# Stores of keys and reciprocal rows moved from the SyncE queue to the ScalarE queue

## The chip, the cores and the metric

The kernel runs on one core of a Trainium2 chip. A core has five engines that run in parallel, each working through its own list of instructions in order: TensorE (PE: matrix products and transposes, results in PSUM), VectorE (DVE), ScalarE (ACT), GpSimd (POOL) and SyncE (SP), which computes nothing and issues DMA transfers between HBM and the on-chip SBUF. Engines wait for one another, and for transfers, through semaphores. A transfer is issued by an instruction in the list of some engine; an instruction whose wait is not yet met holds up all that stands behind it in that list.

The metric is the time of one execution on the device in microseconds (us). The kernel before took 1256.27 us as the median of 3 runs (1255.15 to 1257.36).

## The reference

One layer: `x + W_out(concat[A(h) * silu(g_a), B(h) * silu(g_b)])` with `h = RMSNorm(x)`, 2048 tokens, model width 1024, heads of 64, all in float32. One input projection gives queries, keys, values and gates of both mixers; queries and keys are RMS-normalised per head and rotated.

- Mixer A: 8 query heads on 2 key heads, causal window of 128 tokens, with a learned sink per head. Per query: `m = max(scores, sink)`, `p = exp(s - m)`, `l = sum(p) + exp(sink - m)`, `o = p v / l`.
- Mixer B: 8 heads, three causal patterns (window, dilation): (128, 1), (512, 4), (2048, 16). A query reads the keys `t - j*r`. The three outputs are merged by their softmax denominators: `sum_i w_i o_i / sum_i w_i`, with `w_i = l_i exp(m_i - max m)`.

So at the end of each softmax there is a division by a number per token and head: this is where the reciprocal rows come from.

## The kernel before, in words

**Precision.** A float32 product on TensorE is made of three products of split operands: a high part `h`, rounded by ScalarE as it copies, and a low part `l = x - h`. Each projection so takes three matmuls (`mm3`, L241 to L244), and keys are kept as a high tile `KK` and a low tile `KL` (`klz` in the profile).

**Stages.** `STAGES` (L26) runs through B0 to B3 (two heads of mixer B each), A0 and A1 (four query heads of mixer A each), O0 and O1 (halves of the output projection). By the profile the B stages last until about 665 us, the A stages until about 1070 us, and the output projection makes up the rest. Each stage has four blocks `sb` of 512 tokens, in two halves of 256.

**Projection** (`proj`, L246). For every 128 tokens, 24 matmuls collect into a PSUM tile `pj` (two buffers). ScalarE squares it (L410) and copies V's high part (L411), VectorE makes the rotation's products and V's low part (L311); then `pj` is free. GpSimd adds (L431) and makes the norm factors (L182), VectorE applies them (L447), and ScalarE and GpSimd split the result into high and low (L456 to L459). Loads of x (L148), of weights (L118, L131), rotation tables and scales are issued along the way.

**Finish** (`finish`, L342). Some time later these splits are transposed on TensorE (`qk_transposes`, L463). ScalarE copies out the high keys (L478 into `KK`) and the low keys (L502 into `KL`); GpSimd writes a second ordering of the queries (`qc`, L479). In a B stage the block's queries, high keys, low keys and gates are then stored to HBM (`qd`, `kd`, `ld`, `gd`; L360 to L369), one transfer per head, because the dilated patterns read them back in another order in the next stage. The carried last keys of a block are copied by ScalarE into the next one (L349, L352).

**Attention units.** `units_B`, `units_A` and `units_D` give pieces of work (scores, transposes, products with V, an `after` step) that `advance` (L931) places between the matmuls of the projection. `units_D` holds the dilated patterns of the stage before, for residue r = 0 to 3. Its `load` (L780) reads `qd`, `kd` (L785), `ld` (L788) and `vd` back.

**The reciprocal rows.** At the end of a dilated unit (`after`, L854) and of a pair of A heads (`rows`, L662), the merge weights or reciprocals are worked out as a small tile with one row per token. TensorE transposes it, ScalarE copies it out of PSUM (`rr`: L879 with 16 x 128, L673 with 8 x 128 numbers), and it is stored to a small HBM tensor (`rD`, L881; `rA`, L675). From there it is loaded again as a broadcast over 64 partitions (`Rb`, L890 and L682), and GpSimd multiplies the attention outputs by it (L899, L904; L688). A list `late` of counted-down steps keeps some pieces of other work between the store and the load, and between the load and the use.

**What sets the order.** The program is traced in Python order; a planner (`TileContext(nc, schedule_with_timeline_sim=True)`, L1036) then orders each engine's list by priority and by a simulated timeline, assigns buffers, and adds the semaphores. On the chip each list is run strictly in its planned order. In the kernel before, every transfer is issued by SyncE: one list for loads and stores alike.

## Time and profile before

| | |
|---|---|
| Median of 3 runs | 1256.27 us (1255.15 to 1257.36) |
| Profiled execution | 1261.51 us, of which 1259.4 us are the span from the first to the last instruction |
| TensorE busy | 1174.8 us (93%), mean granted clock 0.969 |
| VectorE, ScalarE, GpSimd busy | 850.7 (68%), 834.7 (66%), 680.4 us (54%) |
| DMA | 220.98 MB in 196883 packets; the queue's packets took 59.3% of the time of 16 DMA engines |
| Stores moved by the change | kd x32 (128 KB each), ld x32 (128 KB), rD x16 (8 KB), rA x16 (4 KB), all on the SyncE queue |

How to read the lines shown below: an engine's row in the page has its busy time, the share of the span and the number of instructions. In rows of waits, "SPq L890 <- DMA rD<-rr: 34.7, 14, 5.3" says that the SyncE queue, at the instruction of line 890, waited for the transfer into rD, 34.7 us in total, 14 times, 5.3 us at the longest. In rows in order of time the first number is the start and the second the duration, both in us; "[7.27 <-DMA Rb<-rD]" is the idle time before it and what ended it. A transfer's row on SPq is its issue: the time for which the instruction occupied SyncE. A row that begins with a time and "DMA" comes from the chain of waits, and shows a transfer from its issue to its landing. Names such as `po<-idr,hl` are output and inputs by the program's tile names.

### The profile page before, as it was taken

The numbers are of one execution on the slowest core, as the hardware profiler recorded it, in microseconds if no ns is written. First come the engines' busy times: TensorE is split into PE (matmuls) and PEld (weight loads), VectorE is DVE, ScalarE is ACT, GpSimd is POOL, SyncE is SP. The second block draws the span as 40 slices with busy tenths as digits, with TensorE's granted clock in tenths as the row PEclk, the third lists the DMA queues.
The fourth block names the chain that finished last, engine by engine and source line by source line (L and its number), as shares of the span: only waits on it lengthen the run. The fifth ranks groups of instructions, "written<-read, shape, count | busy, mean of one in ns | idle before, by whom it ended". The sixth has DMA issues, their size and how long they took to land.

```text
span 1259.4 us, 25438 instructions
## 1 busy us (share of the span) xinstructions
PE 1174.8 (93%) x8328; PEld 1141.3 (91%) x8328; DVE 850.7 (68%) x2288; ACT 834.7 (66%) x2418; POOL 680.4 (54%) x788
## 2 busy tenths in 40 slices
PE   6898979899899798899998999999999999999899
PEld 5898979899799798888997999898899998999898
DVE  5676768678677678776777788789868877522221
ACT  6477868678677687676777677677776776522221
POOL 4886734566645574536576567565655554333122
PEclk9899989999899899899998999999999999999999
DMA  7454677877687667687775764545333225566561
GB/s 215 120 166 127 193 226 212 229 200 212 182 250 207 210 190 201 189 244 204 199 210 172 228 203 143 150 137 167 114 97 94 80 89 165 163 192 211 166 191 69
DMA packets 196883, 220.98 MB, mean 175 GB/s; under 512 B 34312, under 2 KB 143632, under 8 KB 196752
## 3 DMA queue, kind: packets, MB, share of 16 engines
q1 hardware_dynamic: 196752, 219.37, 59.3%
q8 instruction: 66, 1.08, 0.4%
q14 instruction: 65, 0.53, 0.1%
HBM read 164.44 MB, written 54.86 MB: 174 GB/s over the span
## 4 chain that ended last, share of the span: by engine, by line
PE 55%; DMA 16%; DVE 10%; ACT 8%; POOL 6%; issue 3%; SPq 2%; POOLq 0%; ACTq 0%; DVEq 0%
PE pj L244 39%; DMA xs<-in_xT 3%; DMA Rb<-rD 2%; DMA stg<-in_wB 2%; PE po L849 2%; DMA stg<-in_wO 2%; DMA stg<-in_wA 2%; PE sc L590 1%; PE sc L591 1%; PE po L645 1%; PE pt L828 1%; PE po L735 1%; PE pt L719 1%; ACT P L599 1%; DVE ptl L574 1%
## 5 line engine op out<-in xcount | busy, mean ns | idle before, releaser
L244 PE MATMUL pj<-wh,xh 128*128 128x384 f32 (+1 forms) x1008 | 332.8, 332 | 12.2 <-ACT wh L104 5.5
L244 PE MATMUL pj<-wl,xh 128*128 128x384 f32 (+1 forms) x1008 | 334.4, 332 | 0.8 <-DVE wl L102 0.7
L244 PE MATMUL pj<-wh,xl 128*128 128x384 f32 (+1 forms) x1008 | 333.4, 331 | 1.3 <-DVE xl L157 1.3
L157 POOL TENSOR_TENSOR xl<-xs,xh 128x512 fp32r<-128x512 f32 x158 | 210.3, 1341 | 146.3 <-ACT xh L155 136.6
L155 ACT ACTIVATE xh<-xs 128x512 fp32r<-128x512 f32 x252 | 154.5, 629 | 123.6 <-PE pj L244 100.6
L244 PEld LDWEIGHTS pj<-wh,xh 128*128 128x128 f32 x1008 | 194.0, 193 | 15.7 <-ACT wh L104 5.8
L244 PEld LDWEIGHTS pj<-wl,xh 128*128 128x128 f32 x1008 | 194.8, 193 | 3.2 <-DVE wl L102 1.1
L244 PEld LDWEIGHTS pj<-wh,xl 128*128 128x128 f32 x1008 | 194.4, 193 | 3.0 <-DVE xl L157 1.6
L574 DVE TENSOR_TENSOR ptl<-pt,pth 128x512 fp32r<-128x512 f32 (+3 forms) x232 | 142.0, 619 | 35.5 <-ACT pth L573 31.8
L244 PE MATMUL pj<-xh,wgh 128*128 128x256 f32 x496 | 147.7, 298 | 17.9 <-DVE V L311 12.0
L244 PE MATMUL pj<-xh,wgl 128*128 128x256 f32 x496 | 145.8, 294 | 0.0
L244 PE MATMUL pj<-xl,wgh 128*128 128x256 f32 x496 | 145.4, 293 | 0.0
L573 ACT ACTIVATE pth<-pt 128x512 fp32r<-128x512 f32 (+3 forms) x232 | 123.1, 543 | 23.1 <-PE pt L719 8.1
L431 POOL TENSOR_TENSOR t<-t,t 128x256 f32<-128x256 f32 (+1 forms) x96 | 78.1, 814 | 77.9 <-DVE t L422 57.2
L244 PEld LDWEIGHTS pj<-xh,wgh 128*128 128x128 f32 x496 | 97.8, 197 | 19.7 <-ACT klz L502 5.9
L244 PEld LDWEIGHTS pj<-xl,wgh 128*128 128x128 f32 x496 | 97.8, 197 | 0.6
L244 PEld LDWEIGHTS pj<-xh,wgl 128*128 128x128 f32 x496 | 97.4, 196 | 0.9 <-DVE wgl L105 0.2
L814 ACT ACTIVATE P<-P,scD 128x256 f32<-128x256 f32 (+3 forms) x128 | 71.6, 560 | 33.6 <-DVE scD L813 32.9
L157 DVE TENSOR_TENSOR xl<-xs,xh 128x512 fp32r<-128x512 f32 x94 | 76.9, 823 | 21.1 <-ACT xh L155 20.5
L447 DVE TENSOR_TENSOR t<-t,fac 128x256 f32<-128x256 f32 (+1 forms) x96 | 67.4, 710 | 30.8 <-POOL fac L182 23.7
L182 POOL TENSOR_TENSOR fac<-un,mhalf 128x8 f32<-128x8 f32 (+1 forms) x48 | 85.4, 1779 | 2.5
L813 DVE CUSTOM_DVE_ANT_0 P<-sc,mk 128x256 f32<-128x256 f32 (+3 forms) x128 | 61.1, 484 | 32.2 <-PE sc L809 31.5
(188 smaller groups left out, 3082.8 us busy)
## 6 DMA issues: line engine op xcount, KB each, us to landing
xs<-in_xT SPq DMA_DIRECT2D x94, 512.0 KB
xs<-mx SPq DMA_DIRECT2D x32, 512.0 KB
vd<-V SPq DMA_DIRECT2D x64, 128.0 KB
qd<-qc SPq DMA_DIRECT2D x32, 256.0 KB
TT<-tab SPq DMA_DIRECT2D x32, 256.0 KB
cv<-vd SPq DMA_DIRECT2D x32, 256.0 KB
cq<-qd SPq DMA_DIRECT2D x32, 256.0 KB
ck<-kd SPq DMA_DIRECT2D x64, 128.0 KB
```

Source lines behind the costliest of these rows:

```text
L155: nc.scalar.activation(h, f, AF.Copy)
L157: eng.tensor_tensor(l, f, f32(h), op=OP.subtract)
L182: nc.gpsimd.tensor_tensor(y, u, mhalf.to_broadcast([128, n]), op=OP.pow)
L244: nc.tensor.matmul(o, a, b, start=first and n == 0, stop=last and n == 2, skip_group_check=True)
L431: nc.gpsimd.tensor_tensor(t1[:, :n], t1[:, :n], t2[:, :n], op=OP.add)
L447: nc.vector.tensor_tensor(t1v, t1v, fac[:, tt, :, None].to_broadcast([128, nh, 64]), op=OP.mult)
L573: nc.scalar.activation(hi, pt, AF.Copy)
L574: nc.vector.tensor_tensor(lo, pt, f32(hi), op=OP.subtract)
L590: nc.tensor.matmul(sc[:, j, :], q[h // 2][:, h % 2, i, :], kw, start=True, stop=False)
L813: nc.vector.tensor_tensor_reduce(pd, o[:, :m], m2[:, 512 - m:], -0.125, BIG, OP.add, OP.min, nb)
L814: nc.scalar.activation(pd, pd, AF.Exp, bias=nb, scale=-1.0, accum_out=l)
L849: nc.tensor.matmul(po[:, o:o + w], a, b, start=n_ == 0, stop=n_ == len(seq) - 1, skip_group_check=True)
```

## The change

Four of the issuing calls name another engine; nothing else differs. The 32 stores of high keys, the 32 stores of low keys, the 16 stores of merge weights and the 16 stores of A's reciprocals stand in ScalarE's list instead of SyncE's. The transfers themselves, their sizes and their readers are the same. The stores of queries (`qd`) and gates (`gd`), whose last writers are GpSimd and VectorE, and all loads stay with SyncE.

```diff
@@ finish, B stage
             for h in range(2):
                 nc.sync.dma_start(d["q"][h][:, :, cs].rearrange("r p c -> p r c"),
                                   f32(Q[si, sb][1][:, h]))
-                nc.sync.dma_start(d["k"][h][:, :, cs].rearrange("r p c -> p r c"),
+                nc.scalar.dma_start(d["k"][h][:, :, cs].rearrange("r p c -> p r c"),
                                   f32(KK[:64, h, :, 1:5, :]).rearrange("p r i u -> p r (i u)"))
             for h in range(2):
                 hs = slice(64 * h, 64 * h + 64)
-                nc.sync.dma_start(d["l"][:, hs, cs].rearrange("r p c -> p r c"),
+                nc.scalar.dma_start(d["l"][:, hs, cs].rearrange("r p c -> p r c"),
                                   f32(KL[hs, h, :, 1:5, :]).rearrange("p r i u -> p r (i u)"))
@@ rows, A stage
             nc.scalar.activation(rr[:8], pr, AF.Copy)
             d = dram([8, 128], f"rA{si}_{sb}_{p}")
-            nc.sync.dma_start(d, rr[:8])
+            nc.scalar.dma_start(d, rr[:8])
@@ after, dilated unit
                 nc.scalar.activation(rr, pr, AF.Copy)
                 dd = dram([16, 128], f"rD{si}_{r}")
-                nc.sync.dma_start(dd, rr)
+                nc.scalar.dma_start(dd, rr)
```

## The prediction

> **What bounds the kernel now.** I read the page first, then the stages, then what the queue's head and TensorE wait for, and last three places in order of time.

> ```profile
> span 1259.4 us, 25438 instructions
> PE 1174.8 (93%) x8328; PEld 1141.3 (91%) x8328; DVE 850.7 (68%) x2288; ACT 834.7 (66%) x2418; POOL 680.4 (54%) x788
> PE 55%; DMA 16%; DVE 10%; ACT 8%; POOL 6%; issue 3%; SPq 2%; POOLq 0%; ACTq 0%; DVEq 0%
> 0.00:665.00 665.00, 605.76 (x4072) 587.87 (x4073) 476.59 (x1267) 488.32 (x1399) 391.75 (x494) 0.95 0.70 199
> 665.00:1070.00 405.00, 386.87 (x2774) 373.75 (x2774) 319.59 (x922) 295.90 (x921) 237.64 (x255) 0.98 0.47 142
> ```

> TensorE is busy for 93% of the span, so 85 us at most can be won from its idle time. The two rows of stages (columns: length, busy time of PE, PEld, DVE, ACT, POOL, then clock, DMA share, GB/s) put 59 us of it into the four B stages (0 to 665 us) and 18 us into the A stages. ScalarE is 73% busy in both. In the chain the SyncE queue itself has 2%, some 25 us, and DMA in flight 16%: the issuing queue is seldom what is late, but what it issues often is.

> ```profile
> SPq L890 <- DMA rD<-rr: 34.7, 14, 5.3
> SPq L675 <- ACT rr L673: 28.7, 11, 4.6
> SPq L881 <- ACT rr L879: 10.9, 6, 2.6
> POOL o1c L899 <- DMA Rb<-rD: 58.3, 15, 8.2
> PE pj L244 <- DVE V L311: 13.2, 7, 5.7
> PE sc L808 <- DMA ck<-kd: 1.6, 1, 1.6
> ```

> The first three rows are the SyncE queue's waits (us in total, times, longest), the fourth is GpSimd's, the last two are TensorE's. SyncE stands 39.6 us at its head until ScalarE has written a reciprocal row (L675, L881), and then 34.7 us more until that row has landed in HBM, before it issues the broadcast load Rb (L890), for which GpSimd in turn waits 58.3 us.

> **The change, part by part.** First, what moves to ScalarE's instruction stream. Each issue occupies the engine that makes it:

> ```profile
> L362 SPq DMA_DIRECT2D kd<-KK x32: 602/619/1321, 68.2 to 686.5; - x32
> L366 SPq DMA_DIRECT2D ld<-klz x32: 574/598/1777, 69.6 to 687.8; - x32
> L675 SPq DMA_DIRECT2D rA<-rr x16: 284/290/517, 783.7 to 1099.9; - x16
> L881 SPq DMA_DIRECT2D rD<-rr x16: 328/358/660, 207.8 to 863.0; - x16
> ```

> (ns, minimum/median/maximum.) That is 32 x 0.619 = 19.8 us, 32 x 0.598 = 19.1, 16 x 0.290 = 4.6 and 16 x 0.358 = 5.7, together 49.3 us off SyncE and onto ScalarE. No row of before has an issue on ScalarE; from these rows it lies between 0.28 us, the shortest of the four forms, and 1.78 us, the longest. I take the medians, because the work of the issue is the same.

> Second, **what that delays**. Each of the 16 B blocks issues two high-key and two low-key stores: a burst of 2 x 0.619 + 2 x 0.598 = 2.43 us, right behind the copies that fill the key tiles. Three windows of 10 us that begin where these copies end:

> ```profile
> 218.10:228.10 10.00, 10.00 (x66) 9.76 (x65) 6.74 (x23) 7.41 (x26) 7.42 (x10) 1.00 0.86 249
> 391.50:401.50 10.00, 10.00 (x73) 9.83 (x72) 8.81 (x31) 9.88 (x34) 5.04 (x6) 1.00 0.64 184
> 567.30:577.30 10.00, 10.00 (x73) 9.81 (x72) 6.39 (x20) 8.78 (x28) 5.98 (x9) 1.00 0.68 187
> ```

> ScalarE is busy for 7.4, 9.9 and 8.8 of 10 us there, more than its 73%. So a burst delays all that is queued behind it: the splits hl (L456, L457), the carried keys (L349, L352), the exponentials (L599), and the square and V copy (L410, L411), which hold the PSUM tile pj until VectorE's L311 has read it. TensorE waits for that release. Its cover is the time between the release and TensorE's next use of that buffer, two groups later:

> ```profile
> 226.47 0.34 DVE L311 SCALAR_TENSOR_TENSOR V<-pj,rst,V 128x128 fp32r<-128x128 f32 x1
> 229.54 0.28 PE L244 MATMUL pj<-xh,wgh 128*128 128x256 f32 x1
> 396.87 0.34 DVE L311 SCALAR_TENSOR_TENSOR V<-pj,rst,V 128x128 fp32r<-128x128 f32 x1
> 399.43 0.34 PE L244 MATMUL pj<-wh,xh 128*128 128x384 f32 x1
> 575.09 0.34 DVE L311 SCALAR_TENSOR_TENSOR V<-pj,rst,V 128x128 fp32r<-128x128 f32 x1
> 577.93 0.34 PE L244 MATMUL pj<-wh,xh 128*128 128x384 f32 x1
> ```

> The cover is 229.54 - 226.81 = 2.73 us, 399.43 - 397.21 = 2.22 and 577.93 - 575.43 = 2.50, a mean of 2.48 against a burst of 2.43. Bounds for 16 bursts: 0 where all is covered, 16 x 2.43 = 38.9 us where nothing is. Of the three, one is short by 0.21 us. I take 0.25 us a burst, a little more than that, since L311 already ends seven TensorE waits: **+4 us**.

> Third, **the reciprocal rows**. Here two TensorE stalls can be followed back to a late store:

> ```profile
> 402.43 0.25 ACT L879 ACTIVATE rr<-po 16x128 f32<-16x128 f32 x1
> 410.59 0.38 SPq L881 DMA_DIRECT2D rD<-rr  x1
> 411.02 1.36 SPq L760 DMA_DIRECT2D sd<-scB  x3
> 414.08 1.13 SPq L890 DMA_DIRECT2D Rb<-rD  x2
> 418.34 1.29 POOL L899 TENSOR_TENSOR o1c<-o1c,Rb 128x512 f32<-128x512 f32 x1 [7.27 <-DMA Rb<-rD]
> 431.39 2.88 DVE L447 TENSOR_TENSOR t<-t,fac 128x256 f32<-128x256 f32 x2 [5.71 <-POOL fac L182]
> 434.79 1.11 PE L828 MATMUL pt<-idf,P 128*128 128x128 f32 x4 [5.02 <-DVE ptl L574]
> ```

> The row is ready at 402.68, but SyncE, in order behind other waits, stores it at 410.59, 7.9 us late; Rb is issued at 414.08, GpSimd sits 7.27 us, VectorE waits 5.71 us for GpSimd's factors, TensorE 5.02 us. With the store on ScalarE the row has landed long before; SyncE still has the three sd stores ahead, one issue (0.43 us) sooner, and reaches Rb at 411.95, 2.1 us sooner.

> ```profile
> 227.92 0.27 ACT L879 ACTIVATE rr<-po 16x128 f32<-16x128 f32 x1 [2.22 <-PE po L877]
> 234.72 2.94 DMA rD<-rr
> 237.67 0.48 SPq L890
> 241.36 1.29 POOL L899 TENSOR_TENSOR o1c<-o1c,Rb 128x512 f32<-128x512 f32 x1 [7.86 <-DMA Rb<-rD]
> 250.78 0.45 PE L475 MATMUL po<-idr,hl 128*128 128x128 f32 x3 [2.62 <-POOL hl L458]
> ```

> The same again: ready at 228.19, stored at 234.72, Rb at 237.67, which could go at 234.72, 2.95 us sooner, more than the stall of 2.62. Together 2.1 + 2.6 = 4.7: **-5 us**, between 0 (SyncE is late for Rb in any case) and -7.6 (both stalls whole). What is late next is then Rb's own landing. ScalarE's price for these stores, 4.6 + 5.7 us spread over 32 places, I take as covered beside the bursts; if nothing covers it, it is 10 us.

> Fourth, **SyncE's relief**. The 39.6 us at L675 and L881 I count as nothing: the next thing that SyncE has to do for that row is Rb, which needs the landed row, so the wait moves there. The key stores are otherwise: where a B stage ends, the next loads wait for them.

> ```profile
> 513.93 0.38 ACT L478 ACTIVATE KK<-po 128x256 fp32r<-128x256 f32 x1
> 516.29 3.94 DMA kd<-KK
> 520.29 0.49 SPq L785
> ```

> The keys are ready at 514.31, the store leaves at 516.29, the load ck (L785) follows its landing at 520.29. Two microseconds can go; the TensorE row for ck has 1.6 us in all. With 1 to 2 us for everything else that moves up in SyncE: **-3 us**, between 0 and -8, a third of the 25 us that the chain gives to SPq.

> **Sum:** +4 - 5 - 3 = -4 us. The profiled execution took 1261.5 us (span 1259.4 and 2.1 around it), 5.2 above the median of the runs, 1256.3; 1257.5 there is **1252** as a median.

> [...]

> **The rivals.**

> 1. *The wait moves and the burst is covered: no change, 1256 us.* For it: Rb must still be issued by SyncE in order, where L890's wait is already three times L881's, and the mean cover of 2.48 us is the burst. The order of all engines is planned anew, so that the two stalls may recur elsewhere. Against: a late rD costs TensorE twice in one trace.

> 2. *ScalarE's issues outgrow the cover: slower, 1266 us.* Place: the stretch behind the key copies. If an issue takes 0.9 us there, the burst is 3.6 us, 1.1 over the mean cover, and 16 x 1.1 = 18 us less the 8 gained is +10. It decides from 2.48 + 8/16 = 2.98 us a burst, 0.75 us an issue. For it: maxima of 1.32 and 1.78 us in the issue rows, and a ScalarE that is full just there. Against: medians within 4% of the minima.

> 3. *Small stores land sooner from a queue of their own: 1248 us.* In the quiet A stage a row lands far faster:

> ```profile
> 811.41 1.35 DMA rD<-rr
> ```

> That is 1.35 us against 2.94 above (the DMA share is 0.47 against 0.70). If it is SyncE's own backlog that delays them, Rb comes 1.6 us sooner in 16 blocks. Of the GpSimd waits of 7.27 and 7.86 us half reached TensorE; at a sixth of 16 x 1.6 = 26 us that is 4 us more than my sum. Against: if it is the traffic of all 16 DMA engines, a new queue changes nothing. [...]

> **How the numbers follow.** Forecast (1252) 0.33, first rival 0.24, second 0.31, third 0.12. A measurement of this kernel tells 0.2%, 2.5 us, from no change. Faster: forecast and third rival, 0.45; same: 0.24; slower: 0.31. The range goes from 1239 (both gains at their ends, -7.6 - 8, nothing lost) to 1269 (the second rival with some 3 us for a worse order); beyond it lie issues near 1.8 us. The forecast's own range is 1247 to 1254.

> **What would show it.** Right: issues of kd, ld, rD and rA on ScalarE at 0.3 to 0.65 us; rD stored within 0.1 us of L879's end everywhere; GpSimd's wait for Rb well below 58 us; TensorE's waits that end with L311 near 13 us. Wrong: issues of 0.8 us or more on ScalarE, or TensorE waits ended by ScalarE or L311 that grow by over 8 us (second rival); SyncE's wait at L890 and L682 grown by what L881 and L675 lost, GpSimd's wait for Rb as before (first rival); rD landing near 1.4 us in the B stages (third).

## The result and the profile after

The changed kernel takes **1249.86 us** (median of 10 runs, 1243.58 to 1257.63), the kernel before beside it on the same chip 1257.9 (10 runs): a ratio of **0.9932 [0.9906, 0.9958]**, 0.7% or some 8 us faster. In a later comparison the same pair gave 0.9935 [0.9911, 0.9959]. The forecast was 1252 us, a gain of 4.

The profiled execution of after took 1257.63 us, the slowest of its ten runs; a second profile of the same kernel, taken with the last experiments, took 1250.89. Time totals are read from the second, single rows from the first. First the page of after: span, engines, and the two DMA queues (packets, MB, share of 16 engines).

```profile
span 1255.6 us, 25418 instructions
PE 1178.5 (94%) x8328; PEld 1144.0 (91%) x8328; DVE 866.0 (69%) x2288; ACT 830.8 (66%) x2418; POOL 685.6 (55%) x788
q1 hardware_dynamic: 178576, 210.78, 56.1%
q10 hardware_dynamic: 18176, 8.59, 2.6%
```

A second queue has appeared, q10, with 8.59 MB of the 219.4: the 96 stores. The chain of waits does not show the gain: in this profile it can be followed back only to 432.69 us, and over the same stretch DMA has 13.8% of it against 14.5% in before, SyncE's queue 0.8% against 1.2%. The second profile of after:

```profile
span 1249.1 us, 25418 instructions
PE 1172.4 (94%) x8328; PEld 1138.5 (91%) x8328; DVE 864.3 (69%) x2288; ACT 830.8 (67%) x2418; POOL 686.5 (55%) x788
```

TensorE is idle for 76.7 us (1249.1 - 1172.4) against 84.6 before. That is 7.9 us; since this profile lies 1.1 us above its median and that of before 3.6 above its own, some 2.5 of them are the spread of runs.

Next the price of an issue on ScalarE in after (ns, minimum/median/maximum), to be held against the four rows of SyncE in the prediction:

```profile
L362 ACTq DMA_DIRECT2D kd<-KK x32: 582/617/1453, 67.4 to 682.2; - x32
L366 ACTq DMA_DIRECT2D ld<-klz x32: 582/600/2030, 68.8 to 683.6; - x32
L675 ACTq DMA_DIRECT2D rA<-rr x16: 269/270/508, 778.5 to 1096.4; - x16
L881 ACTq DMA_DIRECT2D rD<-rr x16: 314/318/365, 213.6 to 854.8; - x16
```

The medians are those of SyncE within 2 ns for the keys and 20 and 40 ns lower for the rows. The waits of after (us in total, times, longest), SyncE's list, GpSimd, TensorE and ScalarE:

```profile
SPq L682 <- DMA rA<-rr: 28.6, 9, 7.0
SPq L890 <- DMA rD<-rr: 24.7, 13, 3.4
POOL o1c L899 <- DMA Rb<-rD: 25.3, 11, 4.8
POOL o1c L688 <- DMA Rb<-rA: 42.4, 14, 5.8
PE pj L244 <- DVE V L311: 2.8, 6, 0.8
PE sc L808 <- DMA ck<-kd: 3.6, 1, 3.6
ACT ob L566 <- DMA kd<-KK: 6.8, 2, 3.4
ACT klz L502 <- DMA kd<-KK: 1.7, 1, 1.7
```

SyncE no longer stands at L675 and L881 (28.7 and 10.9 us before). At L890 it stands 10 us less, at L682 it stands 28.6 us. GpSimd's wait at L899 has fallen from 58.3 to 25.3 us (25.8 in the second profile); its other wait for the same loads, at L904, has not (16.8 us before, 16.6 and 30.7 in the two profiles of after). TensorE's waits that end with L311 have fallen from 13.2 to 2.8 us (4.3 in the second profile), although each burst of key stores now stands in front of the copies that hold `pj`. The last two rows are new: ScalarE has stood still behind a key store three times, 8.5 us in all.

The rows now leave at once. The two places that the prediction followed are here, in order of time:

```profile
213.28 0.27 ACT L879 ACTIVATE rr<-po 16x128 f32<-16x128 f32 x1
213.58 0.36 ACTq L881 DMA_DIRECT2D rD<-rr  x1
401.16 0.25 ACT L879 ACTIVATE rr<-po 16x128 f32<-16x128 f32 x1
401.44 0.32 ACTq L881 DMA_DIRECT2D rD<-rr  x1
```

From the end of L879 to the store it is 0.03 us in both. Over all 16 rows the mean is 0.13 us (13 of them at 0.03, one at 1.22), against 1.63 in before, where four of them were 3.7 to 7.9 us late. Read this way, the punctual rows look like the gain. The experiments show that it is not so simple.

### The profile page after: what moved, and what is told of

It reads as the page before. It is cut to its first block, busy times and chain, and to the rows that moved or that the text cites. A ratio compares the mean times of both kernels' runs of the same rounds, so it can differ in the third digit from the quotient of the medians.

```text
span 1255.6 us, 25418 instructions
## 1 busy us (share of the span) xinstructions
PE 1178.5 (94%) x8328; PEld 1144.0 (91%) x8328; DVE 866.0 (69%) x2288; ACT 830.8 (66%) x2418; POOL 685.6 (55%) x788
## 3 DMA queue, kind: packets, MB, share of 16 engines
q10 hardware_dynamic: 18176, 8.59, 2.6%
## 4 chain that ended last, share of the span: by engine, by line
PE 35%; DVE 10%; DMA 9%; ACT 5%; POOL 4%; issue 2%; SPq 0%; POOLq 0%; DVEq 0%; ACTq 0%
PE pj L244 26%; ACT P L599 1%; DMA stg<-in_wO 1%; DMA xs<-in_xT 1%; DMA stg<-in_wA 1%; PE po L735 1%; DVE ptl L574 1%; DVE P L598 1%; PE pt L719 1%; DVE t L447 1%; PE po L849 1%; DMA Rb<-rA 1%; POOL fac L182 1%; DVE xl L157 1%; DVE osum L740 1%
## 5 line engine op out<-in xcount | busy, mean ns | idle before, releaser
L244 PE MATMUL pj<-wh,xh 128*128 128x384 f32 (+1 forms) x1008 | 333.7, 334 | 12.5 <-ACT wh L104 6.5
L244 PE MATMUL pj<-wh,xl 128*128 128x384 f32 (+1 forms) x1008 | 334.1, 332 | 4.2 <-DVE xl L157 4.2
L244 PE MATMUL pj<-wl,xh 128*128 128x384 f32 (+1 forms) x1008 | 333.8, 331 | 0.4 <-DVE wl L102 0.4
L157 POOL TENSOR_TENSOR xl<-xs,xh 128x512 fp32r<-128x512 f32 x158 | 216.0, 1377 | 141.9 <-ACT xh L155 139.5
L244 PEld LDWEIGHTS pj<-wh,xh 128*128 128x128 f32 x1008 | 195.1, 194 | 16.5 <-ACT wh L104 5.3
L244 PEld LDWEIGHTS pj<-wh,xl 128*128 128x128 f32 x1008 | 195.0, 194 | 5.7 <-DVE xl L157 4.9
L244 PEld LDWEIGHTS pj<-wl,xh 128*128 128x128 f32 x1008 | 195.3, 194 | 2.1 <-DVE wl L102 0.6
L574 DVE TENSOR_TENSOR ptl<-pt,pth 128x512 fp32r<-128x512 f32 (+3 forms) x232 | 141.5, 619 | 37.3 <-ACT pth L573 34.8
L244 PE MATMUL pj<-xh,wgh 128*128 128x256 f32 x496 | 147.9, 298 | 6.5 <-ACT klz L502 3.2
L244 PE MATMUL pj<-xh,wgl 128*128 128x256 f32 x496 | 145.4, 293 | 0.7 <-DVE wgl L105 0.7
L244 PE MATMUL pj<-xl,wgh 128*128 128x256 f32 x496 | 145.4, 293 | 0.0
L573 ACT ACTIVATE pth<-pt 128x512 fp32r<-128x512 f32 (+3 forms) x232 | 123.5, 542 | 27.0 <-PE pt L719 6.1
L244 PEld LDWEIGHTS pj<-xh,wgh 128*128 128x128 f32 x496 | 98.2, 198 | 9.0 <-ACT klz L502 3.3
L244 PEld LDWEIGHTS pj<-xh,wgl 128*128 128x128 f32 x496 | 97.8, 197 | 1.2 <-DVE wgl L105 0.8
L244 PEld LDWEIGHTS pj<-xl,wgh 128*128 128x128 f32 x496 | 98.2, 198 | 0.5
L157 DVE TENSOR_TENSOR xl<-xs,xh 128x512 fp32r<-128x512 f32 x94 | 81.3, 868 | 17.3 <-ACT xh L155 16.7
L447 DVE TENSOR_TENSOR t<-t,fac 128x256 f32<-128x256 f32 (+1 forms) x96 | 73.0, 774 | 28.9 <-POOL fac L182 24.0
L182 POOL TENSOR_TENSOR fac<-un,mhalf 128x8 f32<-128x8 f32 (+1 forms) x48 | 84.8, 1768 | 2.8
L458 POOL TENSOR_TENSOR hl<-t,hl 128x128 fp32r<-128x128 f32 (+1 forms) x96 | 57.1, 595 | 45.7 <-ACT hl L456 42.6
```

Of the source, the lines that this page charges most:

```text
L157: eng.tensor_tensor(l, f, f32(h), op=OP.subtract)
L182: nc.gpsimd.tensor_tensor(y, u, mhalf.to_broadcast([128, n]), op=OP.pow)
L244: nc.tensor.matmul(o, a, b, start=first and n == 0, stop=last and n == 2, skip_group_check=True)
L447: nc.vector.tensor_tensor(t1v, t1v, fac[:, tt, :, None].to_broadcast([128, nh, 64]), op=OP.mult)
L458: nc.gpsimd.tensor_tensor(lo, t1v[:, :nq], f32(hi), op=OP.subtract)
L573: nc.scalar.activation(hi, pt, AF.Copy)
```

## The experiments

All ratios are against the kernel before, timed in the same comparison. An interval is 95%.

### One part of the change alone

Keys alone (rows stay with SyncE):

```diff
-            nc.scalar.dma_start(d, rr[:8])
+            nc.sync.dma_start(d, rr[:8])
-                nc.scalar.dma_start(dd, rr)
+                nc.sync.dma_start(dd, rr)
```

> Only the 64 key stores (kd and ld) are issued by ScalarE; the rows stay with SyncE. Theory 1: -3 for SyncE's relief and +4 for the bursts on ScalarE, +1 us, ratio 1.001. Theory 2 (SyncE's relief is the gain): -6 to -8 us, ratio 0.994. Theory 3: any value within 0.5%.

Rows alone (keys stay with SyncE), and of these rD alone and rA alone:

```diff
-                nc.scalar.dma_start(d["k"][h][:, :, cs].rearrange("r p c -> p r c"),
+                nc.sync.dma_start(d["k"][h][:, :, cs].rearrange("r p c -> p r c"),
-                nc.scalar.dma_start(d["l"][:, hs, cs].rearrange("r p c -> p r c"),
+                nc.sync.dma_start(d["l"][:, hs, cs].rearrange("r p c -> p r c"),
```

> Only the 32 stores of reciprocal rows (rD and rA) are issued by ScalarE; the key stores stay with SyncE. Theory 1 (my sum: late rows cost TensorE): most of the gain is here, about -5 us, ratio 0.996; GpSimd's wait for Rb from rD falls from 75 us to about 42, as with the whole change. Theory 2 (relief of SyncE by the key stores): nothing, ratio 0.998 to 1.002. Theory 3 (a new plan of the order, by luck): any value within 0.5%, unrelated to GpSimd's wait.

> Only the 16 stores of merge weights (rD) are issued by ScalarE. Theory 1: as with all rows, about -5 us, since A's rows were seldom late (mean 0.5 us against 1.6 us). Theory 2: nothing. Theory 3: any value within 0.5%; then this and the kernel with all rows need not agree.

> Only the 16 rows rA are issued by ScalarE. Theory A: slower than before, 1.003 to 1.005, in the A stages. Theory B: 0.998 to 1.002.

Everything but rA:

```diff
-            nc.scalar.dma_start(d, rr[:8])
+            nc.sync.dma_start(d, rr[:8])
```

> The whole change less one part: A's reciprocal rows (rA) go back to SyncE; keys and rD stay with ScalarE. If rA on ScalarE costs time (theory A, from the 5.3 us that stage A1 takes longer with all rows moved than with rD alone): 3 to 5 us below the whole change, ratio to before 0.989 to 0.991, and GpSimd's wait for Rb from rA back from 42 to about 25 us. If that difference was a matter of the planned order only (theory B): 0.993, as the whole change.

The planner orders every list anew for each variant, so a difference may come from the order alone. One other order was tried: the key stores were only put ahead of the query stores in the program, and all transfers left with SyncE. It is one draw, and sets no bound on what another order could do:

```diff
             for h in range(2):
+                nc.sync.dma_start(d["k"][h] ...)
+            for h in range(2):
                 nc.sync.dma_start(d["q"][h] ...)
-                nc.sync.dma_start(d["k"][h] ...)
```

> No store changes its queue; the two high-key stores of a block stand ahead of its two query stores in the program, all on SyncE, so that the planner makes a new order. Theories 1 and 2: no difference, ratio 0.998 to 1.002. Theory 3: a difference of the size of the change's, 0.4 to 0.8%, of either sign.

Measured, with the mean lateness of the 16 stores of rD (end of L879 to the start of the store's issue, from each trace):

| kernel | median us | ratio | rD late, us |
|---|---|---|---|
| whole change | 1249.86 | 0.9932 [0.9906, 0.9958] | 0.13 |
| keys alone | 1250.55 | 0.9947 [0.9925, 0.9969] | 0.32 |
| keys and rD | 1250.87 | 0.9951 [0.9919, 0.9982] | 0.07 |
| rD alone | 1250.55 | 0.9945 [0.9923, 0.9967] | 0.81 |
| rows alone | 1256.3 | 1.0003 [0.9975, 1.0032] | 1.11 |
| rA alone | 1257.23 | 1.0014 [0.9996, 1.0031] | |
| another order, all on SyncE | 1256.29 | 1.0004 [0.9982, 1.0026] | 1.51 |

In this table all kernels with the keys on ScalarE gain 0.5 to 0.7%, whatever the rows do; of those with the keys on SyncE only rD alone gains.

**Rows moved alone stay late.** In the trace of rD alone, around the same row that the prediction followed at 402.43 us:

```profile
400.53 0.25 ACT L879 ACTIVATE rr<-po 16x128 f32<-16x128 f32 x1
406.75 0.31 ACTq L881 DMA_DIRECT2D rD<-rr  x1
407.11 0.63 ACT L155 ACTIVATE xh<-xs 128x512 fp32r<-128x512 f32 x1 [5.53 <-DMA vd<-V]
```

ScalarE has the row ready at 400.78, and its own store is next in its own list. It leaves only at 406.75, 5.97 us later, and what ended ScalarE's idle time is the landing of a store of V that SyncE issued at 402.14, after the row was ready. With both rows moved it is the same:

```profile
402.67 0.25 ACT L879 ACTIVATE rr<-po 16x128 f32<-16x128 f32 x1
409.84 0.31 ACTq L881 DMA_DIRECT2D rD<-rr  x1
ACT xh L155 <- DMA vd<-V: 6.8, 1, 6.8
```

Here the store is 6.92 us late, against 7.91 in before. In before it stood behind twelve other issues of SyncE; taken out of that list, it waits for a transfer from the same list instead. Lateness alone doesn't decide the time either: rD alone, with this row 5.97 us late, gains 0.55%, and rows alone gain nothing.

**Keys alone make this row punctual**, with the row still issued by SyncE:

```profile
397.95 0.25 ACT L879 ACTIVATE rr<-po 16x128 f32<-16x128 f32 x1
398.23 0.32 SPq L881 DMA_DIRECT2D rD<-rr  x1
POOL o1c L899 <- DMA Rb<-rD: 24.9, 9, 6.0
```

It is 0.03 us late (of the other rows, two are 1.55 and 2.27 us late), and GpSimd's wait for Rb at L899 is 24.9 us, near that of the whole change (25.3); in the view of rD, which counts all waits of L899 for these loads, it is 38.0 us against 27.7, and 60.5 in before. The gain is 0.53% where the whole change has 0.68%, and the intervals overlap: the two are not told apart.

**Where the parts act.** The stages, measured from TensorE's first matmul of one to that of the next, show three things that repeat over kernels (one profile each; columns of the rows as in the prediction). A0, the first stage of mixer A: before, keys alone, after.

```profile
661.10:866.10 205.00, 194.23 (x1372) 187.57 (x1370) 162.17 (x471) 150.65 (x458) 126.33 (x142) 0.98 0.58 172
```

```profile
652.00:850.60 198.60, 189.76 (x1360) 184.29 (x1360) 167.10 (x469) 149.77 (x453) 125.86 (x142) 0.99 0.61 178
```

```profile
659.40:859.10 199.70, 191.89 (x1372) 185.39 (x1370) 161.04 (x468) 151.21 (x460) 124.08 (x140) 0.99 0.59 176
```

In the five profiles with these key stores on ScalarE (after twice, keys alone, keys and rD, and a variant below with the stores placed later), A0 takes 198.6 to 201.5 us, mean 200.4. In the five with the keys on SyncE (before, another order, rows, rD and rA alone) it takes 203.3 to 206.4, mean 204.9. This is **4.5 us**, more than half the gain, and it repeats over four plans on one side and five on the other, which speaks against one lucky order.

A1, before and rows alone:

```profile
866.10:1045.40 179.30, 174.34 (x1260) 168.47 (x1261) 143.82 (x417) 131.94 (x421) 102.77 (x105) 1.00 0.32 101
```

```profile
857.50:1041.90 184.40, 176.18 (x1266) 170.17 (x1265) 148.56 (x421) 133.74 (x425) 105.51 (x105) 0.99 0.31 98
```

In the five of these ten profiles with rA on ScalarE, A1 takes 181.3 to 184.4 us (mean 182.6), in the other five 178.3 to 179.4 (mean 179.0): a **loss of 3.6 us** that goes with rA alone. In the total it is not resolved: keys and rD without rA (0.9951) is no faster than the whole change.

What TensorE waits for changes in the same way in all of these ten profiles. Its waits that end with VectorE sum to 32.3 to 38.3 us (mean 34.7) where the keys are on SyncE and to 19.4 to 25.2 (22.9) where they are on ScalarE; its waits that end with ScalarE to 28.5 to 33.2 (30.9) and to 34.8 to 38.8 (36.3). So moving the key stores takes some 12 us of one kind away and adds some 5 of the other.

B3, rD alone and rows alone:

```profile
489.00:652.20 163.20, 152.53 (x1060) 147.63 (x1058) 123.89 (x330) 125.28 (x365) 99.05 (x122) 0.99 0.78 221
```

```profile
490.40:653.60 163.20, 154.17 (x1058) 149.82 (x1057) 122.27 (x331) 125.20 (x365) 98.16 (x122) 0.97 0.78 219
```

B3 takes 163.2 us in both, against 173.7 in before and 169.7 to 173.2 in the seven other profiles, the two of after among them. So rD alone gains its 0.55% in another place than the keys do, in a stage where the whole change gains almost nothing, and rows alone give the same gain back in B1 (168.9 against 163.5 us) and A1. The sum of the parts, -0.53, -0.55 and +0.14, is -0.94% against a measured -0.68, which the intervals allow; that rD and rA together give nothing (+0.03) where their sum is -0.41% is just outside what they allow.

### The burst, made longer and spread out

The prediction's second term was a burst of four key stores that outgrows a cover of 2.48 us. Three edits test it. First, the same four stores a block, but in blocks 0 to 2 of each B stage put 3, 6, 9 and 12 steps of other work later, one by one:

```diff
+            for n, (fn, h) in enumerate(((k_store, 0), (k_store, 1), (l_store, 0), (l_store, 1))):
+                if sb == 3:
+                    fn(h)
+                else:
+                    late.append([3 + 3 * n, lambda fn=fn, h=h: fn(h)])
```

> The whole change, but in the first three blocks of a B stage the four key stores are not issued one behind another: they are put 3, 6, 9 and 12 steps later among the attention work, still by ScalarE. If the burst behind the key copies costs, as in my second term, this is faster than the whole change by 3 to 8 us, ratio to before 0.987 to 0.991. If ScalarE's issues cost the same wherever they stand: 0.992 to 0.995. If keys that leave later make later work wait: 0.995 or more.

Measured: 1249.22 us, **0.9939 [0.991, 0.9967]**, beside 0.9935 for the whole change in the same comparison (the stores themselves, now in two small functions, are the same). A cost of the burst of four by standing in one place is not seen; twelve runs on either side resolve some 3 us.

Second, four more stores a block of 8 KB each (four of the 64 key rows a time) behind them, into tensors that nobody reads, issued by ScalarE or by SyncE:

```diff
+            for h in range(2):
+                nc.scalar.dma_start(d["k2"][h][:, :4, cs].rearrange("r p c -> p r c"),
+                                  f32(KK[:4, h, :, 1:5, :]).rearrange("p r i u -> p r (i u)"))
+            for h in range(2):
+                nc.scalar.dma_start(d["l2"][h][:, :4, cs].rearrange("r p c -> p r c"),
+                                  f32(KL[64 * h:64 * h + 4, h, :, 1:5, :]).rearrange("p r i u -> p r (i u)"))
```

> The same four small stores a block, issued by ScalarE. The burst is 2.4 + 1.1 = 3.5 us. If ScalarE's issue time and its waits for a transfer that holds the same completion semaphore cost: 16 x 1.1 = 17 us and more above the whole change, ratio 1.006 to 1.015. If the full copies' 63 us came from the traffic: within 3 us of the whole change.

> The whole change, and behind a block's key stores four more stores of 8 KB each, issued by SyncE, into tensors that nobody reads: 64 issues as in the kernel with full second copies on SyncE (which took 24 us more than before), but 0.5 MB instead of 8.4. If issues on SyncE are what costs, by their time in its list (about 0.27 us each, the row of an 8-row store: 17 us) and by the wait for a free completion semaphore: 10 to 20 us above the whole change, ratio to before 1.002 to 1.010. If the traffic of 8 MB was what cost: within 3 us of the whole change, 0.991 to 0.997.

Third, the same with full copies of 128 KB:

```diff
+            for h in range(2):
+                nc.scalar.dma_start(d["k2"][h][:, :, cs].rearrange("r p c -> p r c"),
+                                  f32(KK[:64, h, :, 1:5, :]).rearrange("p r i u -> p r (i u)"))
+            for h in range(2):
+                hs = slice(64 * h, 64 * h + 64)
+                nc.scalar.dma_start(d["l2"][:, hs, cs].rearrange("r p c -> p r c"),
+                                  f32(KL[hs, h, :, 1:5, :]).rearrange("p r i u -> p r (i u)"))
```

> The whole change, and each of the four key stores of a block is issued a second time by ScalarE, into tensors that nobody reads; 8.4 MB more traffic. The burst on ScalarE is 4.9 us instead of 2.4. If the burst eats the cover of 2.5 us (my term of +4 us, and the rival of issues that outgrow the cover): 16 x 2.4 us of the second half lie open, up to 38 us slower than the whole change, ratio to before about 1.02. If ScalarE has more cover than I counted: within 5 us of the whole change, 0.993 to 0.997.

> The whole change, and the same second copies issued by SyncE: its list is as full as before (64 issues more, 39 us), the traffic as in the kernel with the copies on ScalarE, ScalarE's list as in the whole change. If the gain of the key stores is the time of SyncE's list (relief): the gain of 5 us goes, ratio to before 0.998 to 1.001. If the gain is that keys leave earlier, or an order: it stays, 0.993 to 0.995.

The whole change, unaltered, ran beside the spread and the small stores:

> The whole change once more, beside the three others: 0.990 to 0.996 by the first measurement.

| kernel | median us | ratio |
|---|---|---|
| whole change, again | 1249.74 | 0.9935 [0.9911, 0.9959] |
| + 64 small stores, SyncE | 1266.03 | 1.0078 [1.005, 1.0105] |
| + 64 small stores, ScalarE | 1315.0 | 1.0462 [1.0419, 1.0506] |
| + 64 full copies, SyncE | 1279.62 | 1.0194 [1.0167, 1.0221] |
| + 64 full copies, ScalarE | 1317.64 | 1.0498 [1.0463, 1.0533] |

None of these four came out where it was expected but the small stores on SyncE: the two on ScalarE were put at 1.02 at the most, the full copies on SyncE at 1.001.

**On ScalarE it is a cliff.** The first four stores of a block cost less than their leaving SyncE gains, the next four cost 65 us (1315.0 - 1249.74), whether they carry 0.5 MB or 8. The time of the issues doesn't explain it. In the small copies on ScalarE they are

```profile
L371 ACTq DMA_DIRECT2D k2d<-KK x32: 247/418/1201, 69.6 to 737.5; - x32
L374 ACTq DMA_DIRECT2D l2d<-klz x32: 247/248/964, 70.7 to 741.1; - x32
ACT ob L574 <- DMA k2d<-KK: 64.0, 9, 13.9
ACT ob L574 <- DMA ld<-klz: 19.7, 3, 9.6
PE po L857 <- ACT pth L581: 32.4, 9, 9.4
```

32 x 0.418 + 32 x 0.248 = 21.3 us. But ScalarE stands idle for 64.0 + 19.7 us in stretches of 7 us a time (issues among them) that end with a key store or its copy, and with the smaller rows of this kind for 113.6 us, where after had 8.5; and TensorE then waits 32.4 us for ScalarE's copies of the transposed probabilities (L581; the same wait was 0.7 us in after, L573). These waits do not begin with the extra stores: in keys alone ScalarE already stood 23.6 us behind key stores, and TensorE 9.9 us for L573. One such stretch, in order of time:

```profile
176.35 0.63 ACTq L364 DMA_DIRECT2D kd<-KK  x1
177.31 0.30 ACTq L371 DMA_DIRECT2D k2d<-KK  x1
177.55 0.78 ACT L510 ACTIVATE klz<-po 64x256 fp32r<-64x256 f32 x2
177.96 2.20 ACTq L368 DMA_DIRECT2D ld<-klz  x2
180.93 0.25 ACTq L371 DMA_DIRECT2D k2d<-KK  x1
181.22 2.34 ACTq L374 DMA_DIRECT2D l2d<-klz  x2
183.60 0.60 ACT L574 ACTIVATE ob<-po 64x512 f32<-64x512 f32 x1 [5.27 <-DMA k2d<-KK]
```

ScalarE has computed all that these stores need at 178.33, and computes nothing until 183.60. The five issues of these last rows would take 2 x 0.58 + 3 x 0.25 = 1.91 us by the minima (582 and 247 ns); the other 3.4 us are waits in front of them. It is the wait of rD alone again, for transfers and not for data of these stores.

**SyncE's list costs too.** 64 small stores there add 16.3 us (1266.03 - 1249.74). Their issues take 29.0 us of its time (medians 0.29 and 0.37 us), and it stands 27.8 us more in front of them. In before the 64 key stores took far more of the list than the 38.9 us of their medians: 44.9 us of issues, and 33.7 us in which SyncE stood in front of them, nearly all of it ended by ScalarE (the longest of these rows):

```profile
SPq L362 <- ACT xh L155: 9.5, 2, 5.0
SPq L366 <- ACT xh L155: 3.5, 4, 1.7
SPq L362 <- ACT klz L502: 3.4, 5, 1.6
```

So a fuller list costs and an emptier one gains, but not in proportion: 57 us more cost 16.3, 79 us less gain 6.6.

## Why the prediction was right, and where it was not

**Sign, size and range** held: 1249.86 lies in 1239 to 1269, and in the forecast's own range of 1247 to 1254. The gain was 8 us where 4 were worked out. That the sum came so near is in part luck: of the two terms of gain, one had the wrong cause and the other was too small. (The lower end of the range, by its own terms -7.6 and -8, would be 1240.7 and not 1239.)

**The price of an issue** (0.62, 0.60, 0.29 and 0.36 us) was right to 40 ns. Single issues went past the bound of 1.78 us, up to 2.03. With two issuing engines the medians of the key stores are those with one within 2 ns (617 against 619, 600 against 598); their maxima rose (1453 from 1321, 2030 from 1777).

**The burst (+4 us)** had about the right size in the wrong place. TensorE's waits that end with ScalarE grew by some 5 us with the key stores, but not at L311, whose waits fell instead of growing, and not by the four issues standing together, since with the stores spread these waits are the same (35.8 us) and the time too, within some 3 us. What I had not seen is that ScalarE's price is less the length of the issue than the wait in front of it. By the cover, the lengthened bursts (2.43 + 1.33 us over 2.48, 16 times) should have cost 20 us; they cost 65. So what the second rival feared, a ScalarE held up by its stores, exists one doubling further on, but by waits and not by longer issues (in the small copies 21.3 us of issues against 113.6 us for which ScalarE stood idle).

**The late rows (-5 us)** is the step that failed in its cause. Its signs came true in the whole change, but for three rows 0.14, 0.36 and 1.22 us late: rD leaves after 0.13 us in the mean, GpSimd's wait at L899 fell from 58.3 to 25.3. Yet moving the rows was neither enough to make them punctual nor needed for it. Moved alone they stayed up to 7 us late on ScalarE; left with SyncE they were 0.32 us late in the mean as soon as the key stores were gone. And punctual rows aren't worth the 5 us for certain: with the key stores spread the rows are 0.74 us late in the mean and the time is the same, while rD alone (0.81) and rows alone (1.11) differ by 0.6%.

**SyncE's relief (-3 us)** is, by the runs, the term that carried the gain, and it was too small: keys alone give 0.53%, some 6.6 us. It priced the key stores by their issues and the loads behind them, and left out the 33.7 us for which SyncE stood in front of them. That the emptier list is how the key stores gain is argued from the extra stores above; a more fortunate order of the lists is not excluded. The prediction looked for them where a B stage ends, in the load ck; TensorE's row for ck did not fall (3.6 us from 1.6, and without a row in the second profile). 4.5 us came in A0, spread over several of its halves. No single wait carries the gain; as a class it is TensorE's waits that end with VectorE, some 12 us less.

**The first rival** was half right: the 39.6 us at L675 and L881 did move on in the case of A's rows (L682 from 10.3 to 28.6 us), and in the rows alone, at 1.0003, for both (L682 25.3 us, L890 from 34.7 to 46.0). In the whole change it did not for B's (L890 24.7). **The third** has nothing for it: from the store's issue to Rb's issue the mean is 3.60 us, 3.37 before. The landings themselves are seen only where they lie on the chain: 4.10 us in after, once and in the A stage (748.13), 1.35 to 4.27 in before. Beside the time of the issues, the runs show time for which the issuing engine stands still at them: SyncE 33.7 us in front of the key stores in before, ScalarE 8.5 us behind key stores in after.

**What I took at zero** and was not: rA on ScalarE, 3.6 us in A1, with GpSimd's wait for it (L688) at 42.4 us from 26.7 (34.3 to 44.7 in the five profiles with rA on ScalarE that were compared, 23.0 to 32.2 in those without).

**Open:** why B3 gains some 10 us with rD moved and the keys left, and not with both moved. In before one rD of that stage is 5.87 us late, and 0.03 in rD alone and rows alone; but in after it is 0.36 late, and B3 takes 173.2. Open too is whether the key stores cost SyncE by the time of their issues or by the waits in front of them; the extra stores add both. No variant beat the whole change, and it is not resolved from them either: spread (0.9939), keys and rD (0.9951), keys alone (0.9947) and rD alone (0.9945) lie within its interval.

## What to carry to other kernels

Before moving a store to a computing engine, look beyond the length of the issue: list what the engine would have to wait for before it may issue, other queues' transfers among them, because everything it computes stands behind that wait (here 5.53 us for one row in rD alone). A late transfer may be late because of its neighbours in the list and not because of its own place, as rD was (1.63 us in before, 0.32 with the key stores gone); the experiment that tells is to move the neighbours and leave it. And check the parts alone even when every announced sign comes true: here the sign (punctual rows) and the gain went with one part, the key stores, and nothing shows that the one made the other.

## What the runs showed of the hardware

**Issues wait for transfers of other queues.** The planner gives every transfer one of eight completion semaphores in turn, whichever engine issues it (in before and in after each serves 142 transfers), and most issues (945 of 1136 in the program of before, 85 of ScalarE's 96 in that of after) wait for their own semaphore, that is until the transfer before them with the same one, eight places earlier in the program, has landed. In the planned list of ScalarE with the small stores, 63 of the 64 small stores carry such a wait (this is the program's rule, not the chip's); the first four:

```
104 L371 DMA k2d0_346<-KK_256 4x4x128 [waits DMAHW4_49]
105 L371 DMA k2d0_346<-KK_256 4x4x128 [waits DMAHW5_49]
106 L374 DMA l2d0_347<-klz0_89 4x4x128 [waits DMAHW6_49]
107 L374 DMA l2d0_347<-klz0_89 4x4x128 [waits DMAHW0_49]
```

This is what the trace of rD alone shows as "5.53 <-DMA vd<-V" in front of a ScalarE that needed nothing of `vd`: in its plan the store of that row shares its semaphore with that store of V. So that store, given to ScalarE, still waited for how far SyncE had come: for a store issued there at 402.14. On SyncE such a wait delayed transfers (in before 2.9 us, three times, in front of the stores sd of L760, until a load of x with the same semaphore had landed); on ScalarE it delayed arithmetic, the 5.53 us. That the cliff comes from these waits alone is argued from the rows above; a kernel with more semaphores was not tried.

```profile
425.80:428.80 3.00, 3.00 (x21) 2.93 (x20) 0.00 (x0) 1.63 (x5) 3.00 (x6) 1.00 0.47 140
432.80:439.60 6.80, 4.81 (x19) 4.71 (x20) 4.41 (x17) 4.34 (x16) 3.75 (x7) 0.50 0.93 282
```

```profile
244.00:247.00 3.00, 2.39 (x15) 1.87 (x14) 2.81 (x7) 2.30 (x6) 2.88 (x3) 1.00 0.96 271
252.00:255.30 3.30, 3.30 (x19) 3.30 (x17) 1.85 (x7) 2.23 (x6) 3.30 (x5) 0.50 0.85 226
```

In the slow window the projection's matmuls are 0.52 us long instead of 0.34, and back to back they begin 0.32 us apart instead of 0.17:

```profile
427.75 0.34 PE L244 MATMUL pj<-wh,xh 128*128 128x384 f32 x1
438.80 0.52 PE L244 MATMUL pj<-wh,xh 128*128 128x384 f32 x1
```

By these distances some 46% of the busy time in the slow window is lost; as an estimate, a stall of 2.6 us so costs TensorE another 1.5 us (of the 3.30 in which it was busy), one of 5 us another 2.2 (of 4.81). The shortest of these 11 stalls lasted 2.62 us, and the one that was not followed by half the clock 2.11 us; in the first profile of after one of 2.05 us (410.64) was followed by it. In all, TensorE ran at half clock for 79 us of the span in before and 79 and 61 us in the two of after, and between runs of one kernel the time falls by some 7.2 us for 0.01 of mean granted clock (30 runs of before, correlation -0.61): over a third of the variance of these runs goes with the clock.
